# Batched 64x64 matmul: the second half of the transposes moved ahead of the multiplication, and a cast moved from VectorE to GpSimd

## The chip, the cores and the metric

The kernel runs on one core of one Trainium2 chip. The metric is the device time of that core in microseconds (us). All timed runs used below are marked fast, which keeps them apart from runs in a slower state, unless said otherwise. The profile's span is 1.8 to 1.9 us shorter than the device time of the same run.

## The reference

```python
a, b: 1024 x 64 x 64, float32
return np.matmul(a, b).astype(np.float32)
```

That is 16.8 MB for each of a, b and the output: 50.3 MB to be moved for a small amount of arithmetic.

## The kernel before

The batch is cut into 16 b tiles (t, 64 matrices each) and 8 a tiles (s, 128 matrices each). For each tile, a is turned to bf16, transposed on TensorE, spread into a block-diagonal operand on VectorE, and multiplied with b, which is cast to bf16. ScalarE and VectorE copy the results out of PSUM (the memory that TensorE writes to), and GpSimd issues the stores.

Three DMA queues matter. GpSimd's queue (queue 0 of the profile) carries three quarters of each a tile, cast to bf16 by the transfer itself, and all stores. SyncE's queue (queue 1, "SP") carries the fourth quarter in fp32 and the even b tiles, ScalarE's queue (queue 10, "ACT") the odd b tiles.

```python
    def load_a(s):
        a_sb = a_pool.tile([128, 3, 16, 64], bf16, name="a_sb")
        for h in range(3):
            nc.gpsimd.dma_start(out=a_sb[:, h, :, :]..., in_=a_v[s, h])     # casts on the way
        a_raw = a_pool.tile([128, 16, 64], fp32, name="a_raw")
        nc.sync.dma_start(out=a_raw[:]..., in_=a_v[s, 3])
    def load_b(t):                                  # 512-byte pieces in HBM
        queue = nc.scalar if t % 2 else nc.sync
        queue.dma_start(out=b_sb[:], in_=b_v[t])
    def regroup(s):
        # ... (the first a tile is handled apart)
            nc.vector.tensor_copy(a_bf[:, :, 0:3, :], cast_sb[:]...)
            nc.vector.tensor_copy(a_bf[:, :, 3, :], raw[:])
    # ... transpose, spread, cast, multiply, store
    # before the loop: load_first_a(), load_b(0..3), load_a(1), load_a(2)
        for t in range(n_t):
            s, half = t // 2, t % 2
            # ... spread(t + 1), cast(t + 1), load_b(t + 4), load_a(s + 4)
            multiply(t)
            if t == 0:
                regroup(1)
                load_a(A_AHEAD)          # tile 3
                load_a(A_AHEAD + 1)      # tile 4
                transpose(1, 0)
            elif t == 1:
                regroup(2)
            elif half == 0 and s + 2 < n_s:
                regroup(s + 2)
            if half == 0 and s + 1 < n_s:
                transpose(s + 1, 1)
            if half == 1 and s + 2 < n_s:
                transpose(s + 2, 0)
            if t >= HOLD - 1:
                store(t - HOLD + 1)
```

The order is written by hand, and each engine takes its instructions in that order.

Of the kernel before, what the change touches and what calls it, by code (L numbers as in the profile page):

```python
# [13 lines left out]
def kernel(  # L14
# [14 lines left out]
    nc = tc.nc  # L29
# [4 lines left out]
    n_t, n_s = B // 64, B // 128  # L34
# [29 lines left out]
# [4 lines that stand above are left out]
            nc.gpsimd.dma_start(  # L68
                out=a_sb[:, h, :, :].rearrange("p v k -> p (v k)"), in_=a_v[s, h]
            )  # L70
        a_raw = a_pool.tile([128, 16, 64], fp32, name="a_raw")
        nc.sync.dma_start(out=a_raw[:].rearrange("p v k -> p (v k)"), in_=a_v[s, 3])  # L72
        a_tiles[s] = a_sb, a_raw

    def load_first_a():

        raw = [
            o_pool.tile([128, 8, 2, 2, 64], fp32, name="o_sb")[:].rearrange(
                "p gh j wl n -> p (gh j wl n)"
            )  # L80
            for _ in range(2)
        ]
        parts = [raw[h % 2][:, 1024 * (h // 2) : 1024 * (h // 2) + 1024] for h in range(4)]
        for h in range(4):
            (nc.scalar if h % 2 else nc.sync).dma_start(out=parts[h], in_=a_v[0, h])  # L85
        a_tiles[0] = parts

    def load_b(t):
        b_sb = b_pool.tile([128, 16, 128], fp32, name="b_sb")
        queue = nc.scalar if t % 2 else nc.sync  # L90
        queue.dma_start(out=b_sb[:], in_=b_v[t])  # L91
        b_tiles[t] = b_sb

    def regroup(s):
        a_sb = a_tiles.pop(s)
        a_bf = work.tile([128, 16, 4, 64], bf16, name="a_bf")
        if s == 0:
            for h in range(4):
                copy = nc.scalar.copy if h % 2 else nc.vector.tensor_copy
                copy(a_bf[:, :, h, :], a_sb[h].rearrange("p (v k) -> p v k", v=16))  # L100
        else:
            cast_sb, raw = a_sb
            nc.vector.tensor_copy(  # L103
                a_bf[:, :, 0:3, :], cast_sb[:].rearrange("p h v k -> p v h k")
            )
            nc.vector.tensor_copy(a_bf[:, :, 3, :], raw[:])  # L106
        abf_tiles[s] = a_bf
        at_tiles[s] = work.tile([128, 2, 32, 2, 4, 4], fp32, name="at_sb")

    def transpose(s, j):  # L110
        a_cols = abf_tiles[s][:].rearrange("p v h k -> p v (h k)").bitcast(fp32)
        for wl in range(2):
            at_ps = t_psum.tile([128, 4, 128], fp32, name="at_ps")
            for vo in range(4):
                nc.tensor.transpose(  # L115
                    at_ps[:, vo, :], a_cols[:, 4 * vo + 2 * j + wl, :], identity[:]
                )
            nc.scalar.copy(  # L118
                at_tiles[s][:, j, :, wl, :, :],
                at_ps[:].rearrange("p vo (g mp) -> p g mp vo", mp=4),  # L120
            )

    def spread(t):
        half = slice(16 * (t % 2), 16 * (t % 2) + 16)
        bd = bd_tiles[t % N_BD]
        for h in range(4):
            rows = slice(32 * h, 32 * h + 32)
            nc.vector.tensor_copy(  # L128
                bd[rows, :, :, :, h, :].rearrange("p j g wl mo -> p j (g wl) mo"),
                at_tiles[t // 2][rows, :, half, :, :, :].rearrange(  # L130
                    "p j g wl mp vo -> p j (g wl) (mp vo)"
                ),
            )

    def cast(t):
        b_bf = work.tile([128, 16, 128], bf16, name="b_bf")
        b_sb = b_tiles.pop(t)
        if t < n_t - 1:
            (nc.vector.tensor_copy if t else nc.scalar.copy)(b_bf[:], b_sb[:])  # L139
        else:  # L140
            for gq in range(4):
                rows = slice(4 * gq, 4 * gq + 4)
                if gq % 2:
                    nc.vector.tensor_copy(b_bf[:, rows, :], b_sb[:, rows, :])
                else:
                    nc.scalar.copy(b_bf[:, rows, :], b_sb[:, rows, :])  # L146
        bbf_tiles[t] = b_bf
# [5 lines left out]
    def multiply(t):  # L153
        at_bd = bd_tiles[t % N_BD][:].rearrange("p j g wl h mo -> p j g (wl h mo)")
        at_bd = at_bd.bitcast(bf16).rearrange("p j g (c u) -> p j g c u", u=2)
        b_bf = bbf_tiles.pop(t)
        last = t == n_t - 1
        o_sb = o_pool.tile([128, 8, 2, 2, 64], fp32, name="o_sb")

        def put(lo, n):  # L160
            nc.gpsimd.dma_start(  # L161
                out=o_v[t, :, lo : lo + n, :],
                in_=o_sb[:, lo : lo + n].rearrange("p gh j wl n -> p (gh j wl n)"),
            )

        def evacuate(o_ps, gh, n, copies):

            for par in range(2):
                for wl in range(2):
                    src = o_ps[64 * wl : 64 * wl + 64, :, par, :, :]  # L170
                    dst = o_sb[64 * par : 64 * par + 64, gh : gh + n, :, wl, :]
                    copies[2 * par + wl](dst, src)  # L172

        for half in range(2):
            if not last:
                o_ps = o_psum.tile([128, 4, 2, 2, 64], fp32, name="o_ps")
            for g8 in range(8):
                if last and g8 % 4 == 0:
                    o_ps = t_psum.tile([128, 2, 2, 2, 64], fp32, name="at_ps")
                g = 8 * half + g8  # L180
                gl = (g8 % 4 if last else g8) // 2
                for j in range(2):
                    for u in range(2):
                        nc.tensor.matmul(  # L184
                            o_ps[:, gl, g % 2, j, :],
                            at_bd[:, j, g, :, u],
                            b_bf[:, g, 64 * u : 64 * u + 64],
                            start=(u == 0),
                            stop=(u == 1),
                        )  # L190
                if last and g8 % 4 == 3:
                    copy = nc.scalar.copy if g8 == 3 else nc.vector.tensor_copy
                    evacuate(o_ps, g // 4 * 2, 2, [copy] * 4)
            if not last:
                copies = [nc.scalar.copy] * 4
                if half and t % 2:
                    copies[2:] = [nc.vector.tensor_copy] * 2
                evacuate(o_ps, 4 * half, 4, copies)
        if last:
            held[t] = [lambda q=q: put(2 * q, 2) for q in range(4)]  # L200
        else:
            whole = t < n_t - 2
            held[t] = [lambda q=q: put(q, 8 if whole else 4) for q in ([0] if whole else [0, 4])]

    with tc.manual_schedule():
        load_first_a()

        nc.vector.memset(warm[:, 0:1], 0.0)
        nc.scalar.copy(warm[:, 1:2], warm[:, 0:1])  # L209
        load_b(0)  # L210
        load_b(1)
        nc.vector.memset(bd_tiles[0][:], 0.0)  # L212
        make_identity(nc, identity)
        nc.gpsimd.memset(bd_tiles[1][:, 0], 0.0)
        load_a(1)
        load_b(2)
        nc.gpsimd.memset(bd_tiles[1][:, 1], 0.0)  # L217
        load_a(2)
        regroup(0)
        transpose(0, 0)  # L220
        transpose(0, 1)
        load_b(3)
        spread(0)
        cast(0)
        for t in range(n_t):
            s, half = t // 2, t % 2
            if t + 1 < n_t:
                spread(t + 1)
                cast(t + 1)
            if t + B_AHEAD < n_t:  # L230
                load_b(t + B_AHEAD)
            if half == 0 and 0 < s < n_s - 1 - A_AHEAD:
                load_a(s + 1 + A_AHEAD)
            multiply(t)
            if t == 0:
                regroup(1)
                load_a(A_AHEAD)
                load_a(A_AHEAD + 1)
                transpose(1, 0)
            elif t == 1:  # L240
                regroup(2)
            elif half == 0 and s + 2 < n_s:
                regroup(s + 2)
            if half == 0 and s + 1 < n_s:
                transpose(s + 1, 1)
            if half == 1 and s + 2 < n_s:
                transpose(s + 2, 0)
            if t >= HOLD - 1:
                store(t - HOLD + 1)
        for t in range(n_t - HOLD + 1, n_t):  # L250
            store(t)
# [30 lines left out]
```

## Time and profile before

| | before |
|---|---|
| device time, median | 135.62 us |
| span of the profiled run | 133.8 us |
| busy: TensorE, VectorE, ScalarE, GpSimd | 49, 70, 66, 28% of the span |
| bytes in and out | 33.55 + 16.78 MB, 376 GB/s over the span |

The lines of the page that show the bound stand in the prediction. Two more views matter for what happened; I should have weighed them before I predicted. The first is GpSimd's timeline up to 26 us, its DMA issues alone: start, length, engine, line, operation, tiles, count, and in brackets the idle time before it.

```profile
3.00 1.78 POOL L68 DMA_DIRECT2D a_sb<-in_a_dram  x3
...
6.50 2.94 POOL L68 DMA_DIRECT2D a_sb<-in_a_dram  x5
11.65 0.54 POOL L68 DMA_DIRECT2D a_sb<-in_a_dram  x1 [2.21 <-DMA a_sb<-in_a_dram]
23.88 1.61 POOL L68 DMA_DIRECT2D a_sb<-in_a_dram  x3 [11.70 <-DVE a_bf L103]
```

The loads of tile 2, and right behind them those of tile 3 (the last two of the five and the one at 11.65), are issued by 12.2 us, far ahead of their use. And the very first load, issued at 3.00 us on an empty queue 0, has its first packet at 7.11 us by the packets' records, 4.1 us later; the prediction takes no account of that. The second is the table of stretches (its columns head the one in the prediction; the last two are the busy share of the DMA engines and the GB/s that the profile counts).

```profile
5.00:7.00 2.00, 0.00 (x0) 0.00 (x0) 1.82 (x2) 0.23 (x1) 2.00 (x2) 1.00 1.02 416
25.00:28.00 3.00, 3.00 (x27) 2.99 (x25) 0.00 (x0) 2.93 (x6) 0.49 (x1) 1.00 1.07 306
```

From 5 to 7 us queue 0 has not begun, and the two other queues move rows of 4 KB at 416 GB/s. From 25 to 28 us all three queues work; 306 is counted, with the casting loads at their 2 bytes written. By the packets' records, with 4 bytes read, it is 401.

### The profile page before, as it was taken

To read this page: it belongs to the slowest core of one execution; us is meant where nothing else is said; L and a number is where in the kernel's file an instruction comes from. 1 tells how busy PE (TensorE), PEld (TensorE's weight loads), DVE (VectorE), ACT (ScalarE), POOL (GpSimd) and SP (SyncE) were. 2 spreads that over 40 slices of the span, in tenths; PEclk is the share of its full clock that TensorE was granted. 3 is DMA by queue.
4 is the path that set the end of the run, shared out by engine and by line. 5 is a ranking of instruction groups with operands and counts; after the bars stand their busy time and mean duration, and the time that the engine had idled before them with its cause. 6 is when DMAs were issued, how large, how long until landed. Compare 5 with 4: busy or idle time off the path is not lost.

```text
span 133.8 us, 2832 instructions
## 1 busy us (share of the span) xinstructions
PE 65.8 (49%) x1152; PEld 61.6 (46%) x1152; DVE 93.9 (70%) x120; ACT 87.7 (66%) x161; POOL 37.4 (28%) x49
## 2 busy tenths in 40 slices
PE   0005505990078524976398276839535860974000
PEld 0005305990078513966396266738525750963000
DVE  5920299208997039998998999999889949979000
ACT  3134504999137994399779979967994999498000
POOL 8981000420082150307023021404200430426400
PEclk9999999999558965589658977977997798555555
DMA  3999999999999999999999999999999999999991
GB/s 75 359 335 312 305 315 312 306 304 305 306 307 384 365 310 310 393 391 396 317 306 355 403 388 371 318 301 374 393 390 391 393 396 404 404 387 356 337 334 51
DMA packets 17485, 45.01 MB, mean 336 GB/s; under 512 B 1088, under 2 KB 1088, under 8 KB 17472
## 3 DMA queue, kind: packets, MB, share of 16 engines
q0 software_dynamic: 7440, 22.28, 54.8%
q1 hardware_dynamic: 5520, 13.11, 27.0%
q10 hardware_dynamic: 4512, 9.44, 18.6%
q8 instruction: 9, 0.15, 0.4%
q14 instruction: 4, 0.03, 0.1%
HBM read 33.55 MB, written 16.78 MB: 376 GB/s over the span
## 4 chain that ended last, share of the span: by engine, by line
DMA 35%; SPq 27%; ACT 10%; issue 8%; DVE 7%; POOL 3%; PE 3%; POOLq 1%; ACTq 1%; DVEq 0%
SPq L72 23%; DMA a_raw<-in_a_dram 18%; DMA b_sb<-in_b_dram 17%; ACT o_sb L172 8%; DVE at_bd L128 4%; SPq L91 3%; POOL out_dram L161 3%; DVE b_bf L139 3%; PE o_ps L184 3%; ACT at_sb L118 2%; SPq L85 1%; ACT b_bf L146 1%; POOLq L277 1%; ACTq L91 1%; POOLq L161 0%
## 5 line engine op out<-in xcount | busy, mean ns | idle before, releaser
L172 ACT COPY o_sb<-o_ps 64x512 f32<-64x512 f32 x106 | 61.6, 581 | 15.6 <-PE o_ps L184 14.4
L184 PEld LDWEIGHTS <-at_bd 128*128 128x128 bf16 x1024 | 42.8, 114 | 38.0 <-DVE b_bf L139 27.3
L184 PE MATMUL o_ps<-b_bf,at_bd 128*128 128x64 bf16 x960 | 41.2, 214 | 33.3 <-DVE b_bf L139 24.5
L128 DVE COPY at_bd<-at_sb 32x1024 f32<-32x1024 f32 x64 | 45.7, 714 | 16.8 <-ACT at_sb L118 15.1
L161 POOL DMA_DIRECT2D out_dram<-o_sb x20 | 20.3, 1018 | 62.0 <-ACT o_sb L172 24.8
L115 PE MATMUL at_ps<-identity,a_bf 128*128 128x128 f32 x128 | 23.2, 346 | 21.9 <-ACT a_bf L100 11.5
L115 PEld LDWEIGHTS at_ps<-identity,a_bf 128*128 128x128 f32 x128 | 19.7, 184 | 22.1 <-issue 19.3
L118 ACT COPY at_sb<-at_ps 128x512 f32<-128x512 f32 x32 | 17.5, 590 | 8.2 <-PE at_ps L115 7.9
L68 POOL DMA_DIRECT2D a_sb<-in_a_dram x21 | 13.0, 634 | 25.2 <-DVE a_bf L103 19.4
L139 DVE CAST b_bf<-b_sb 128x2048 bf16<-128x2048 f32 x14 | 17.9, 1277 | 1.1 <-DMA b_sb<-in_b_dram 0.7
L172 DVE COPY o_sb<-o_ps 64x512 f32<-64x512 f32 x14 | 9.7, 690 | 0.3
L106 DVE CAST a_bf<-a_raw 128x1024 bf16<-128x1024 f32 x7 | 4.8, 687 | 6.3 <-DMA a_raw<-in_a_dram 6.3
L103 DVE COPY a_bf<-a_sb 128x3072 bf16<-128x3072 bf16 x7 | 6.7, 952 | 0.0
L100 ACT CAST a_bf<-o_sb 128x1024 bf16<-128x1024 f32 x2 | 2.1, 1044 | 5.5 <-DMA o_sb<-in_a_dram 5.5
L139 ACT CAST b_bf<-b_sb 128x2048 bf16<-128x2048 f32 x1 | 1.9, 1898 | 4.0 <-DMA b_sb<-in_b_dram 4.0
L100 DVE CAST a_bf<-o_sb 128x1024 bf16<-128x1024 f32 x2 | 2.5, 1249 | 2.6 <-DMA o_sb<-in_a_dram 2.6
L172 DVE COPY o_sb<-at_ps 64x256 f32<-64x256 f32 x8 | 3.4, 422 | 1.0 <-PE at_ps L184 0.9
L184 PE MATMUL at_ps<-b_bf,at_bd 128*128 128x64 bf16 x64 | 3.6, 242 | 1.0 <-DVE at_bd L128 1.0
L212 DVE MEMSET at_bd<- 128x4096 f32 x1 | 3.5, 3472 | 0.8 <-issue 0.8
L172 ACT COPY o_sb<-at_ps 64x256 f32<-64x256 f32 x8 | 2.9, 367 | 0.1
L209 ACT ACT_TABLE_LOAD x1 | 1.3, 1283 | 2.3 <-issue 2.3
L217 POOL MEMSET at_bd<- 128x2048 f32 x1 | 1.8, 1849 | 0.0
(12 smaller groups left out, 5.6 us busy)
## 6 DMA issues: line engine op xcount, KB each, us to landing
out_dram<-o_sb POOLq DMA_DIRECT2D x14, 1024.0 KB, 22.9
a_sb<-in_a_dram POOLq DMA_DIRECT2D x21, 256.0 KB, 17.8
a_raw<-in_a_dram SPq DMA_DIRECT2D x7, 512.0 KB, 24.1
o_sb<-in_a_dram ACTq DMA_DIRECT2D x2, 512.0 KB, 7.4
o_sb<-in_a_dram SPq DMA_DIRECT2D x2, 512.0 KB, 6.3
out_dram<-o_sb POOLq DMA_DIRECT2D x2, 512.0 KB, 9.4
out_dram<-o_sb POOLq DMA_DIRECT2D x4, 256.0 KB, 8.1
b_sb<-in_b_dram SPq DMA_DIRECT2D x8, 0.5 KB, 22.0
```

The lines of the kernel that those rows point to most:

```text
L68: nc.gpsimd.dma_start(out=a_sb[:, h, :, :].rearrange("p v k -> p (v k)"), in_=a_v[s, h])
L72: nc.sync.dma_start(out=a_raw[:].rearrange("p v k -> p (v k)"), in_=a_v[s, 3])
L91: queue.dma_start(out=b_sb[:], in_=b_v[t])
L103: nc.vector.tensor_copy(a_bf[:, :, 0:3, :], cast_sb[:].rearrange("p h v k -> p v h k"))
L106: nc.vector.tensor_copy(a_bf[:, :, 3, :], raw[:])
L115: nc.tensor.transpose(at_ps[:, vo, :], a_cols[:, 4 * vo + 2 * j + wl, :], identity[:])
L118: nc.scalar.copy(at_tiles[s][:, j, :, wl, :, :], at_ps[:].rearrange("p vo (g mp) -> p g mp vo", mp=4),)
L128: nc.vector.tensor_copy(bd[rows, :, :, :, h, :].rearrange("p j g wl mo -> p j (g wl) mo"), at_tiles[t // 2][rows, :, half, :, :, :].rearrange(
L139: (nc.vector.tensor_copy if t else nc.scalar.copy)(b_bf[:], b_sb[:])
L161: nc.gpsimd.dma_start(out=o_v[t, :, lo : lo + n, :], in_=o_sb[:, lo : lo + n].rearrange("p gh j wl n -> p (gh j wl n)"),)
L172: copies[2 * par + wl](dst, src)
L184: nc.tensor.matmul(o_ps[:, gl, g % 2, j, :], at_bd[:, j, g, :, u], b_bf[:, g, 64 * u : 64 * u + 64], start=(u == 0), stop=(u == 1),)
```

## The change

It takes the casts of the fp32 quarter off VectorE, which is over 90% busy in the middle, and brings both halves of a tile's transposes together, ahead of the even tile's multiplication, so that the block-diagonal copies wait less for them.

```diff
-            nc.vector.tensor_copy(a_bf[:, :, 3, :], raw[:])
+            nc.gpsimd.tensor_copy(a_bf[:, :, 3, :], raw[:])
 ...
+            if half == 0 and 0 < s < n_s - 1:
+                transpose(s + 1, 1)
             multiply(t)
             if t == 0:
                 regroup(1)
                 load_a(A_AHEAD)
                 load_a(A_AHEAD + 1)
                 transpose(1, 0)
+                transpose(1, 1)
 ...
-            if half == 0 and s + 1 < n_s:
-                transpose(s + 1, 1)
```

## The prediction

> **What bounds the kernel now.** I read the page's slices first, to see which resource is full from end to end, then the DMA queues, then the stretches, then the chain and the waits, to see whether any engine's idle time reaches that resource.
>
> ```profile
> DVE  5920299208997039998998999999889949979000
> PEclk9999999999558965589658977977997798555555
> DMA  3999999999999999999999999999999999999991
> GB/s 75 359 335 312 305 315 312 306 304 305 306 307 384 365 310 310 393 391 396 317 306 355 403 388 371 318 301 374 393 390 391 393 396 404 404 387 356 337 334 51
> ...
> q0 software_dynamic: 7440, 22.28, 54.8%
> q1 hardware_dynamic: 5520, 13.11, 27.0%
> q10 hardware_dynamic: 4512, 9.44, 18.6%
> ...
> HBM read 33.55 MB, written 16.78 MB: 376 GB/s over the span
> ## 4 chain that ended last, share of the span: by engine, by line
> DMA 35%; SPq 27%; ACT 10%; issue 8%; DVE 7%; POOL 3%; PE 3%; POOLq 1%; ACTq 1%; DVEq 0%
> ```
>
> The DMA row is what matters: the sixteen DMA engines are over 90% busy in 38 of the 40 slices, all but the first and the last; no compute engine comes near that. The three queues' packet times add to 54.8 + 27.0 + 18.6 = 100.4% of the engines' span. The GB/s row looks uneven, 305 in the first third and 395 later, but that is a matter of counting: queue 0 carries the three quarters of a that are cast on the way, and the profile counts their 2 bytes written, not the 4 read. Loads and stores together are 33.55 + 16.78 = 50.33 MB, the page counts 45.01, and the difference, 5.3 MB, is about the 21 casting loads at 256 KB each. Where queue 0 casts, and each queue gives its share, 305 counted is some 370 to 400 moved. So the byte rate is nearly level.
>
> ```profile
> core 0: us, PE busy (x) PEld busy (x) DVE busy (x) ACT busy (x) POOL busy (x), PEclk, DMA share, GB/s
> ...
> 50.00:65.00 15.00, 9.46 (x152) 8.59 (x150) 13.97 (x19) 10.83 (x21) 3.69 (x4) 0.73 1.05 367
> 65.00:80.00 15.00, 10.48 (x194) 9.72 (x195) 14.16 (x19) 12.26 (x23) 2.86 (x4) 0.73 1.05 356
> ...
> 110.00:120.00 10.00, 5.34 (x97) 5.18 (x98) 8.97 (x12) 7.96 (x15) 2.59 (x3) 0.62 1.03 400
> 120.00:130.00 10.00, 1.85 (x35) 1.69 (x32) 3.38 (x8) 3.31 (x9) 3.60 (x5) 0.50 1.00 345
> ```
>
> This is the table of stretches. VectorE is 93% busy between 50 and 80 us, so one could take it for the bound; but the DMA share is 1.0 or above (packets overlap a little) in every stretch. In the last one the compute engines do next to nothing, and the DMA engines are still full, with stores alone, at 345 GB/s. The timeline of GpSimd has its last store issued at about 124.4 us, 9 us before the end: at some 340 GB/s, and with about 2 us of landing, that is a backlog of some 2.3 MB which was already waiting when the compute ended. A compute that ended some us earlier or later would leave the same bytes to be moved.
>
> **What the Trainium skill says.** (1) "DMA: Bandwidth & Descriptors", section "Queues, rings and completion order": each DMA engine takes its queues in turn, a packet at a time. The trace agrees in its sums: a late or empty queue hands its turns to the others, and the DMA row never drops. (2) The same page, section "Bandwidth", gives about 358 GB/s as one core's HBM share and 435 as the ceiling of the fabric. The trace has 376 over the span and 390 to 404 in mixed slices, so it is above the first and 7% below the second: little is left to be had. (3) "GPSIMD Engine Reference", section "Engine selection": a one-input elementwise operation runs roughly at line rate on GpSimd. The trace has no such copy on GpSimd; its memset of 2048 fp32 took 1.85 us, 0.9 ns an element. (4) "SBUF — State Buffer", section "SBUF: two separate sides": a VectorE instruction in a two-port mode and a GpSimd instruction exclude each other for their whole length. The block-diagonal copies (1024 elements in about 0.69 us) and the casts of b (2048 in 1.23 us) differ by 0.53 ns an element, which I take for that mode; whether they hold GpSimd up no run shows yet.
>
> **The change, part by part.**
>
> ```profile
> L128 DVE COPY at_bd<-at_sb 32x1024 f32<-32x1024 f32 x64 | 45.7, 714 | 16.8 <-ACT at_sb L118 15.1
> L161 POOL DMA_DIRECT2D out_dram<-o_sb x20 | 20.3, 1018 | 62.0 <-ACT o_sb L172 24.8
> ...
> L106 DVE CAST a_bf<-a_raw 128x1024 bf16<-128x1024 f32 x7 | 4.8, 687 | 6.3 <-DMA a_raw<-in_a_dram 6.3
> ```
>
> Each row: busy us and mean ns, then the idle time before and what ended most of it.
>
> *The cast moves.* VectorE loses 7 casts x 0.687 = 4.8 us and a wait of 6.3 us (one: from 42.7 to 48.95 us it stands before the cast of the third a tile, whose load is late). GpSimd gains 7 casts. By the memset, 1024 elements are 0.9 us, with fixed cost 1.1, and up to 2.2 if VectorE's copies hold the port: 8 to 15 us, against 37.4 of 133.8 us busy. By throughput that is free. GpSimd's queue, however, is in order, and the waits come along: the cast of tile 1 now stands ahead of the three casting loads of tile 3 (issued from about 9 us before), and cannot run before its load lands; VectorE ran it at 23.5. So those loads issue at about 25 to 27 us. Queue 0 has the six loads of tiles 1 and 2 before them, 3.1 MB read; at half of 400 GB/s from about 9 us on that lasts until some 25 us. A gap of 0 to 3 us in queue 0 is the result, and the two other queues have work to fill it. The next cast waits for a load used at 36.9 before, so the first store slips from 28.7 to about 38 us; it was queued behind casting loads anyway. The third waits until about 49 us, so the store issued at 39.7 slips to about 50, behind a store and 1.5 MB of loads that keep queue 0 busy past it.
>
> *The transposes move.* Nothing is added: 128 transposes and 32 copies out of PSUM stay. Those of the second half now stand ahead of the multiplication of the even tile, so VectorE's copies, which waited 15.1 us in 6 waits for them, wait less: I take 8 to 10 us off, since the first waits are for loads. In return, each even multiplication stands behind 8 transposes (8 x 0.13 to 0.24 us, 1 to 2 us) and its evacuation behind two more copies of 0.59 us: six times some 2 to 3 us later on TensorE and ScalarE. These cost nothing where the loads decide.
>
> *Sum.* On VectorE, 4.8 + 6.3 + 8 to 10 = about 20 us of work and waits go, of 134. If compute set the end I would have to take off perhaps 10 us. But the sum for the end is the DMA one: about 2.6 us until data flows, 50.33 MB at 376 to 400 GB/s = 126 to 134 us, a last landing of about 2. The change moves no byte, changes no descriptor and no queue. What it can alter is the mix: while stores run beside loads the rate is about 393, stores alone go at 345 at the end. If the loads end 2 us earlier because the compute frees b's buffers earlier, some 0.4 to 0.7 MB more of stores goes at the slow rate: 0.7 / 0.345 - 0.7 / 0.393 = 0.2 us more. If stores come earlier and mix, it is 0.2 us less. Net: 0 to within 0.5 us. I put 135.6 us.
>
> **The rivals.** *(A) VectorE is the true pace, and the kernel gets faster.* For it: 93% busy in the middle, and the chain of waits goes through VectorE, PE and ScalarE from 49 to 65 and from 100 to 113 us. Against it: at that time the DMA row is full, and the chain is mostly DMA and its queue (35 + 27%). It would give 130 to 133 us, no less, since 50.33 MB at 400 GB/s and 4.6 us of ends are 130.4. *(B) GpSimd's casts hold up loads and stores, and the DMA engines run dry.* For it: the order above, and GpSimd's loads and stores wait for earlier transfers too. Against it: transfers take 18 to 24 us from issue to landing, so each queue holds as much in hand, and one queue's gap is another's turn. Should it dry up once at 25 to 30 us and once at 45 to 50, that is 2 to 5 us: 138 to 141. *(C) The lock between GpSimd and VectorE* slows both by up to 7 x 1.5 = 10 us: off the bound too, so under 0.5 us at the end.
>
> **Range and chances.** The before runs lie within 0.05 us, so the spread is that of my argument: 0.5 us for the mix, one small gap of about 1 us upward, one better mix of about 1 us downward. That is 134.5 to 136.9 us. Two per cent are 2.7 us: faster needs rival A nearly to its limit, 0.03; slower needs B, 0.05; within 2%, 0.92.
>
> **What would show it.** Right: the DMA row still 9 from the second slice to the last but one; VectorE's busy time near 89 us, its wait for ScalarE's transposes under 7 us, the 6.3 us wait for the fp32 quarter gone from VectorE and found on GpSimd; GpSimd's cast at 0.9 to 2.2 us; the stretch from 120 to 130 us at 335 to 360 GB/s. Wrong: a DMA slice under 9 between 20 and 60 us (B), or a last store issued after 128 us with the DMA row falling before it. Bytes over span gives the mean rate, 376 GB/s now: over 384 in the changed kernel would say that the mix of loads and stores matters more than I think, and is where I would have been wrong upward.

## The result

| | before | changed |
|---|---|---|
| device time, median | 135.62 us | 137.44 us |
| all runs | 135.51 to 135.66 | 136.81, 137.43, 137.44, 137.44 |
| span of the profiled run | 133.8 us | 134.9 us |

The ratio is 1.0123, with a 95% interval of 1.0095 to 1.0152. Ratios in this document are the mean time of one kernel's fast runs over that of the other's of the same rounds, so they are not quite the ratio of the medians. The change made the kernel 1.2% slower: within 2%, but clear of noise, and outside my range of 134.5 to 136.9. The profiled run of the changed kernel is the quickest of its four.

The same lines of the page as in the prediction, for the changed kernel:

```profile
DVE  5930597019997819998999999797299998963000
DMA  3999999999999999999999999999999999999991
GB/s 80 369 328 310 306 316 312 316 288 305 307 304 306 403 351 308 314 404 395 382 324 311 338 396 400 381 304 307 379 387 392 399 404 399 387 358 340 341 334 57
...
HBM read 33.55 MB, written 16.78 MB: 373 GB/s over the span
...
DMA 49%; SPq 17%; issue 12%; DVE 6%; POOL 4%; PE 2%; ACT 1%; POOLq 1%; DVEq 0%
```

The DMA row is the same as before, 9 in every slice but the first and the last, and yet the mean rate fell from 376 to 373 GB/s. The only mark in the first third is 288 in the ninth slice (27.0 to 30.4 us), which looks harmless beside 305. Then the two groups that the change touches (busy us, mean ns of one, idle before and what ended it):

```profile
L128 DVE COPY at_bd<-at_sb 32x1024 f32<-32x1024 f32 x64 | 50.5, 789 | 14.9 <-ACT at_sb L118 12.4
...
L106 POOL CAST a_bf<-a_raw 128x1024 bf16<-128x1024 f32 x7 | 7.4, 1056 | 33.6 <-DMA a_raw<-in_a_dram 33.6
```

The cast is on GpSimd, 1.06 us each, and GpSimd now stands 33.6 us before it, waiting for the fp32 quarter. VectorE's copies became longer, 789 ns for 714. GpSimd's timeline shows where the longest of those waits is:

```profile
6.48 1.86 POOL L68 DMA_DIRECT2D a_sb<-in_a_dram  x3
22.50 1.12 POOL L106 CAST a_bf<-a_raw 128x1024 bf16<-128x1024 f32 x1 [14.16 <-DMA a_raw<-in_a_dram]
23.56 3.23 POOL L68 DMA_DIRECT2D a_sb<-in_a_dram  x6
```

For 14.16 us GpSimd waits for the first fp32 quarter, and the loads of tile 3 stand behind it: their issue moved from about 8.3 to 23.56 us. And the stretches:

```profile
25.00:28.00 3.00, 2.31 (x49) 2.21 (x48) 0.00 (x0) 2.92 (x7) 1.79 (x4) 1.00 1.05 298
110.00:118.00 8.00, 4.12 (x82) 3.83 (x83) 7.16 (x10) 7.79 (x15) 2.73 (x3) 0.67 1.02 396
120.00:130.00 10.00, 0.69 (x13) 0.53 (x10) 2.42 (x6) 1.33 (x4) 2.85 (x4) 0.50 1.01 344
```

298 against 306 between 25 and 28 us looks like 3%. It is 25%. In the kernel before, half of the traffic in this stretch is casting loads that are counted at half of their size; in the changed kernel there are none, so all is counted. I worked the bytes out from the packets' records, queue by queue, with the casting loads at their size in HBM, the chip's main memory:

```
GB/s moved, in us from the span's start
             24   25   26   27   28   29      queue 0's last packet of tile 2, first of tile 3
before      402  401  402  401  400  390      24.7   24.5
changed     402  317  290  290  346  396      24.8   28.2
```

(Each column is one us.) For 3.4 us queue 0 has nothing to move. SP and ACT have work, their packets follow each other without a pause, and the DMA engines are counted as 1.05 busy; but they move only 290 GB/s. Summed over the columns the changed kernel is 355 KB short of the kernel before, which at 401 GB/s is 0.9 us, of a difference of 1.2 us between the two profiled spans (134.94 and 133.78).

The second, smaller item is at the end. While queue 0 is empty, the loads of the other queues run ahead (0.91 MB of them from 24 to 27 us, before 0.64), so the last load lands sooner (109.1 us, before 110.5), and more stores are left to run alone: 8.34 MB against 7.48. Stores alone begin at some 400 GB/s and fall to 345 (the stretches of 110 to 118 and 120 to 130 us). 0.86 MB at 344 in place of 400 GB/s is 0.35 us. The two estimates add to 1.25 us, against 1.16 measured.

A running total of the same records says where the loss arises. Against the kernel before, the changed kernel is 27 KB ahead at 24 us and 329 KB behind at 30; at 40, 50 and so on to 100 us it is 263 to 342 KB behind, at 110 us 272, and at 125 us 434. So nothing between 30 and 110 us adds to it.

### The profile page after: what moved, and what is told of

It reads as the page before. It is cut to its first block, busy times and chain, and to the rows that moved or that the text cites. A ratio compares the mean times of both kernels' runs of the same rounds, so it can differ in the third digit from the quotient of the medians.

```text
span 134.9 us, 2848 instructions
## 1 busy us (share of the span) xinstructions
PE 63.8 (47%) x1152; PEld 60.6 (45%) x1152; DVE 93.9 (70%) x113; ACT 87.6 (65%) x161; POOL 44.3 (33%) x56
## 4 chain that ended last, share of the span: by engine, by line
DMA 49%; SPq 17%; issue 12%; DVE 6%; POOL 4%; PE 2%; ACT 1%; POOLq 1%; DVEq 0%
DMA a_sb<-in_a_dram 20%; DMA a_raw<-in_a_dram 17%; SPq L72 14%; DMA out_dram<-o_sb 12%; POOL out_dram L161 4%; DVE at_bd L128 3%; SPq L91 2%; DVE b_bf L139 2%; PE o_ps L184 2%; DVE o_sb L172 1%; SPq L85 1%; ACT o_sb L172 1%; POOLq L278 1%; POOL a_sb L68 0%; POOLq L161 0%
## 5 line engine op out<-in xcount | busy, mean ns | idle before, releaser
L128 DVE COPY at_bd<-at_sb 32x1024 f32<-32x1024 f32 x64 | 50.5, 789 | 14.9 <-ACT at_sb L118 12.4
L184 PEld LDWEIGHTS <-at_bd 128*128 128x128 bf16 x1024 | 42.0, 112 | 39.2 <-DVE b_bf L139 23.5
L115 PE MATMUL at_ps<-identity,a_bf 128*128 128x128 f32 x128 | 21.0, 334 | 20.4 <-ACT a_bf L100 10.9
L115 PEld LDWEIGHTS at_ps<-identity,a_bf 128*128 128x128 f32 x128 | 19.0, 178 | 20.7 <-issue 11.9
L106 POOL CAST a_bf<-a_raw 128x1024 bf16<-128x1024 f32 x7 | 7.4, 1056 | 33.6 <-DMA a_raw<-in_a_dram 33.6
L139 DVE CAST b_bf<-b_sb 128x2048 bf16<-128x2048 f32 x14 | 17.2, 1227 | 1.0 <-DMA b_sb<-in_b_dram 0.6
L103 DVE COPY a_bf<-a_sb 128x3072 bf16<-128x3072 bf16 x7 | 7.2, 1023 | 3.5 <-DMA a_sb<-in_a_dram 3.4
```

Source lines behind the costliest of these rows:

```text
L103: nc.vector.tensor_copy(a_bf[:, :, 0:3, :], cast_sb[:].rearrange("p h v k -> p v h k"))
L106: nc.gpsimd.tensor_copy(a_bf[:, :, 3, :], raw[:])
L115: nc.tensor.transpose(at_ps[:, vo, :], a_cols[:, 4 * vo + 2 * j + wl, :], identity[:])
L128: nc.vector.tensor_copy(bd[rows, :, :, :, h, :].rearrange("p j g wl mo -> p j (g wl) mo"), at_tiles[t // 2][rows, :, half, :, :, :].rearrange(
L139: (nc.vector.tensor_copy if t else nc.scalar.copy)(b_bf[:], b_sb[:])
L184: nc.tensor.matmul(o_ps[:, gl, g % 2, j, :], at_bd[:, j, g, :, u], b_bf[:, g, 64 * u : 64 * u + 64], start=(u == 0), stop=(u == 1),)
```

## The experiments

The theory that I took into the experiments (G): the loss comes from the gap in queue 0, which GpSimd's first cast causes by standing before the loads of tile 3; the transposes, and the six later casts, cost nothing. The rivals: the loss comes from the transposes, by way of the stores at the end (T), or from the exclusion between GpSimd's and VectorE's instructions (L).

A correction ahead: in the first two sets of expectations I gave the packets' times 1.8 us too late, because I had not lined them up with the page's clock. Where they say that the gap begins at 26.5 us and that a packet comes 6.3 us after its issue, the right readings are 24.8 us and 4.7 us. Nothing in the verdicts hangs on it, as both ends moved together.

### 1. The transposes alone

```diff
 # changed kernel
-            nc.gpsimd.tensor_copy(a_bf[:, :, 3, :], raw[:])
+            nc.vector.tensor_copy(a_bf[:, :, 3, :], raw[:])
```

> Only the transposes move; the cast of the fp32 quarter stays on VectorE. Theory G (gap): the loss comes from GpSimd's first cast, which stands before the three casting loads of the third a tile and leaves queue 0 empty from about 26.5 to 30 us; without that cast no slice between 20 and 35 us shows a fall, and the time is 135.3 to 136.0 us. Rival T (tail): the loads end earlier because the transposes come earlier, so more stores run alone at some 340 GB/s at the end; then 136.5 to 137.4 us. Rival L (lock, VectorE slowed by GpSimd's casts): 135.3 to 136.0, and the block-diagonal copies are back at about 714 ns.

Measured: 135.47 us against 135.58 for the kernel before on the same chip; ratio 0.9989 (0.9975 to 1.0002). The rate at 25 to 28 us is 402 GB/s by the packets' records. The moved transposes do no harm, and no good that can be told from noise: T falls.

### 2. The casts alone

```diff
 # kernel before
-            nc.vector.tensor_copy(a_bf[:, :, 3, :], raw[:])
+            nc.gpsimd.tensor_copy(a_bf[:, :, 3, :], raw[:])
```

> Only the cast moves to GpSimd; the transposes stay where they were before. G: the whole loss, 136.7 to 137.5 us, and the gap at 26 to 30 us. T: the loads end as before, 135.4 to 136.0 us. L: 136.7 to 137.5 with the copies at about 790 ns, but no fall in the DMA rate at 26 to 30 us.

Measured: 137.31 us, ratio 1.0126 (1.0111 to 1.0141): the whole loss. Queue 0 is empty from 24.9 to 29.2 us, and the records give 315, 290, 290 and 291 GB/s from 25 to 29 us. The two groups:

```profile
L128 DVE COPY at_bd<-at_sb 32x1024 f32<-32x1024 f32 x64 | 49.6, 776 | 22.5 <-ACT at_sb L118 20.7
...
L106 POOL CAST a_bf<-a_raw 128x1024 bf16<-128x1024 f32 x7 | 8.4, 1207 | 31.7 <-DMA a_raw<-in_a_dram 31.7
```

VectorE's copies are slower here as well (776 ns), so this run alone leaves both G and L.

### 3. The changed kernel with the loads of tile 3 first

```diff
 # changed kernel
             if t == 0:
+                load_a(A_AHEAD)
                 regroup(1)
-                load_a(A_AHEAD)
                 load_a(A_AHEAD + 1)
```

> The changed kernel with one line moved: the third a tile's loads are issued ahead of the first tile's cast, so GpSimd still does all seven casts. G: the gap at 26 to 30 us is gone, and with it about 1 us: 135.6 to 136.5 us. T or L: nothing gained, 136.8 to 137.5 us.

Measured: 135.8 us, ratio 1.0006 (0.999 to 1.0021): the loss is gone, but for 0.2% at most. GpSimd still does all seven casts, VectorE's copies still take 778 ns, and GpSimd still waits, now 36.5 us, for the fp32 quarters. But the loads of tile 3 are now ahead of the first of these waits, as its timeline shows:

```profile
6.50 2.93 POOL L68 DMA_DIRECT2D a_sb<-in_a_dram  x5
11.57 0.54 POOL L68 DMA_DIRECT2D a_sb<-in_a_dram  x1 [2.14 <-DMA a_sb<-in_a_dram]
22.62 1.45 POOL L106 CAST a_bf<-a_raw 128x1024 bf16<-128x1024 f32 x1 [10.51 <-DMA a_raw<-in_a_dram]
```

Queue 0 does not run dry, and the records give 402, 402 and 400 GB/s from 25 to 28 us. So L falls, and so does any cost of GpSimd's waits as such.

### 4. The first cast alone

```diff
 # kernel before
-            nc.vector.tensor_copy(a_bf[:, :, 3, :], raw[:])
+            (nc.gpsimd if s == 1 else nc.vector).tensor_copy(a_bf[:, :, 3, :], raw[:])
```

> The kernel before with the first of the seven casts alone on GpSimd. G: this one cast stands before the loads, so nearly the whole loss: 136.3 to 137.4 us with the gap at 26 to 30 us. T: 135.4 to 135.9 us. L: a seventh of the loss, 135.6 to 135.9 us.

Measured: 137.5 us, ratio 1.0138 (1.0122 to 1.0155). One cast of the seven brings the whole loss. From GpSimd's timeline:

```profile
22.84 1.58 POOL L106 CAST a_bf<-a_raw 128x1024 bf16<-128x1024 f32 x1 [14.49 <-DMA a_raw<-in_a_dram]
24.37 3.23 POOL L68 DMA_DIRECT2D a_sb<-in_a_dram  x6
```

The loads of tile 3 issue at 24.37 us, and their first packet moves at 29.3. VectorE's copies are at 713 ns as before, so there is a full loss without their slowing. The two estimates for this run: 427 KB fewer in the gap (1.06 us at 401 GB/s) and 8.88 MB of stores alone, 1.4 MB more than before (0.6 us at some 340 in place of 400 GB/s), together about 1.7 of the 1.8 us between the spans (135.6 and 133.8).

### 5. and 6. No cast at all, but GpSimd kept busy

These hold the loads of tile 3 back by idle work, five or eight memsets, in the kernel before.

```diff
 # kernel before; idle is a scratch tile of 128 x 2048 fp32
                 regroup(1)
+                for _ in range(5):          # or 8
+                    nc.gpsimd.memset(idle[:], 0.0)
                 load_a(A_AHEAD)
```

> The kernel before, with no cast moved, but GpSimd filled with five idle memsets of about 1.85 us ahead of the third a tile's loads, which so issue at about 17.6 us instead of 8.3. In the runs so far the first packet of these loads came about 6.3 us after their issue when queue 0 had run empty, so here it would come at about 24, before queue 0 runs dry at 26.5. Theory G (only an empty queue 0 costs): no gap, 135.3 to 136.0 us. Rival (any delay of GpSimd's loads, or GpSimd's work itself, costs): 136.2 to 137 us.

> The same with eight idle memsets: issue at about 23.2 us, as behind the cast in the changed kernel, first packet at about 29.5. G: the gap from 26.5 to 29.5 us and the whole loss without any cast on GpSimd, 136.7 to 137.6 us. Rival (the cast itself, by its port or its waits): 135.3 to 136.0 us.

Measured: with five, 135.57 us, ratio 1.0 (0.9984 to 1.0017); with eight, 136.97 us, ratio 1.0103 (1.0078 to 1.0128). The timelines of GpSimd, first with five, then with eight:

```profile
8.22 10.15 POOL L239 MEMSET idle<- 128x2048 f32 x5
18.32 2.15 POOL L69 DMA_DIRECT2D a_sb<-in_a_dram  x3
```

```profile
8.21 17.03 POOL L239 MEMSET idle<- 128x2048 f32 x8
25.19 2.15 POOL L69 DMA_DIRECT2D a_sb<-in_a_dram  x3
```

Issued 10 us late, at 18.32, the loads still come in time for queue 0, and nothing is lost. Issued at 25.19, their first packet moves at 29.9 us, the records show 316, 290, 290 and 290 GB/s from 25 to 29 us, and most of the loss is there without any cast on GpSimd. (VectorE's copies are slowed by the memsets, to 817 ns on average, but experiment 4 has the full loss with copies of 713 ns.) What counts is when the loads are issued against the moment at which queue 0 runs dry, not what GpSimd does meanwhile.

In these runs, and in the ones before, an issue on an empty queue 0 is followed by its first packet after 4.7 to 5 us (changed 23.56 and 28.23, casts alone 24.20 and 29.15, first cast 24.37 and 29.26, eight memsets 25.19 and 29.94). The first load of the kernel before took 4.1 us (3.00 and 7.11). In the changed kernel the loads were issued 1.3 us before queue 0 ran dry, and 1.3 us is less than 4.7: the gap of 3.4 us is the difference.

### 7. and 8. b in long pieces

To see why SP and ACT alone move only 290 GB/s, I gave b the same bytes in 8 KB pieces in the kernel before and in the changed one. Their outputs are wrong, which doesn't matter for the times.

```diff
-    b_v = b.rearrange("(t g h) (kp u) n -> t (h kp) g (u n)", h=4, g=16, u=2)
+    b_v = b.rearrange("(t q) (r k) n -> t (q r) (k n)", q=64, r=2)
 ...
-        queue.dma_start(out=b_sb[:], in_=b_v[t])
+        queue.dma_start(out=b_sb[:].rearrange("p g n -> p (g n)"), in_=b_v[t])
```

> The kernel before with b read in 8 KB contiguous pieces per partition instead of 512 B ones; the same bytes into the same tile, so a wrong result on purpose. Reference for the next run: 134.5 to 136 us.

> The changed kernel with b read in 8 KB pieces, wrong result on purpose. If the gap costs because the b loads, left alone with 512 B pieces, move only 290 GB/s instead of 402 (theory P, pieces), then here the rate from 27 to 30 us stays at 380 or above although queue 0 is empty, and the time is within 0.5 us of the run before it. Rival Q (two queues alone cannot fill the engines, whatever the pieces): the rate falls to about 290 to 320 here too, and the time is 1.2 to 2 us above the run before it.

Measured: 134.07 and 134.59 us; ratios to the kernel before 0.9888 (0.9855 to 0.9922) and 0.9923 (0.9899 to 0.9947). This pair did not decide the question. With longer packets the two other queues take a greater share, queue 0 has work of tile 2 until 33 us in place of 25, the first fp32 quarter lands at about 18 (the cast of the changed kernel starts at 18.21), and so there is no gap at all: the rate at 25 to 28 us is 409 to 418 GB/s in both. It shows only that without the gap the changed kernel is some 0.5 us from the other, with intervals that overlap, and that long pieces are worth about 1% here.

### 9. and 10. Queue 0 kept empty at the start

Here the two other queues are alone for longer, by idle work ahead of the first loads of GpSimd, with b in 512 B and in 8 KB pieces. The times are not compared.

```diff
 # kernel before; the second run has the diff of 7 and 8 as well
+        for _ in range(5):
+            nc.gpsimd.memset(idle[:], 0.0)
         load_a(1)
```

> The kernel before with five idle memsets on GpSimd ahead of its very first loads, so that queue 0 is empty until about 17 us and the SP and ACT queues work alone: first on rows of 4 KB (the first a tile), then on b in 512 B pieces. Both theories expect some 415 GB/s while the 4 KB rows go, as in the kernel before at 5 to 7 us. Theory P (the pieces of b are what is slow): about 290 GB/s from 9 us until queue 0 starts. Rival Q (two queues without queue 0 are slow in any case): no step down at the change from a to b. (Times of the packets in my earlier expectations were read 1.8 us late.)

> The same with b read in 8 KB pieces, wrong result on purpose. P: 400 GB/s or more from 9 us until queue 0 starts. Q: about 290 to 320, as in the run with 512 B pieces.

The stretches, first with 512 B pieces, then with 8 KB pieces (nothing casts in them, so the GB/s are true):

```profile
5.00:7.00 2.00, 0.00 (x0) 0.00 (x0) 1.96 (x2) 0.44 (x1) 1.94 (x2) 1.00 1.02 418
9.00:11.00 2.00, 0.31 (x2) 0.34 (x3) 0.49 (x1) 1.04 (x1) 2.00 (x1) 1.00 1.07 296
11.00:13.00 2.00, 2.00 (x11) 2.00 (x10) 0.00 (x0) 0.92 (x2) 1.94 (x2) 1.00 1.04 286
```

```profile
5.00:7.00 2.00, 0.00 (x0) 0.00 (x0) 2.00 (x2) 0.72 (x1) 1.94 (x2) 1.00 1.03 424
9.00:11.00 2.00, 0.00 (x0) 0.00 (x0) 0.48 (x1) 0.92 (x1) 2.00 (x1) 1.00 1.00 424
11.00:13.00 2.00, 1.78 (x9) 1.81 (x10) 0.00 (x0) 0.71 (x2) 1.94 (x2) 1.00 0.99 412
```

In the first row of each, SP and ACT move the 4 KB rows of the first a tile at 418 and 424 GB/s. When they come to b, the rate falls to 296 and 286 with 512 B pieces, and stays at 424 and 412 with 8 KB pieces. The DMA share is 0.99 to 1.07 throughout. Two queues can fill the engines (Q falls); it is b's short pieces, with nothing longer between them, that move at 290 GB/s (P). The other layout changes more than the pieces: by the packets' records b moves in packets of 2,048 bytes with the first and of 8,192 with the second, and the order of addresses differs. Which of these counts, the runs do not separate; "short pieces" stands for all of them here. Why pieces of 512 B are slow alone and do no harm when packets of queue 0 come between them, these runs do not show.

### 11. and 12. Fewer bytes for the last, slow phase

If the second item of the sum is real, a kernel whose stores get more turns earlier should gain. I gave late b tiles to the SP queue, so that ACT's queue is empty for a while and queue 0 is served more often.

```diff
 # changed kernel with the cast on VectorE (experiment 1)
-        queue = nc.scalar if t % 2 else nc.sync
+        queue = nc.scalar if t % 2 and t not in (13,) else nc.sync     # or (9, 13)
```

> The kernel with only the transposes moved, and one late b tile (the fourteenth) loaded on the SP queue in place of the ACT queue, so that ACT's queue is empty for a while, queue 0 gets more turns, and the stores move ahead of the loads. Theory S (the last stores, alone, go at 345 GB/s, so fewer bytes left for that phase cost less time): store bytes after the last load fall from about 7.8 to 7.2 MB, 135.2 us. Without S: no change, 135.5 us, or slower if the later loads hold up the compute.

> The same with two late b tiles (the tenth and the fourteenth) on the SP queue. S: store bytes after the last load about 6.6 MB, 134.9 us. Without S: 135.5 us or slower.

Measured: with one tile moved, 134.89 us against 135.53, ratio 0.996 (0.9945 to 0.9976); with two, 139.7 us, ratio 1.0309 (1.0295 to 1.0323). With one, the last load lands at 114.9 us in place of 109.7, and 5.74 MB of stores are left for the lonely phase in place of 7.78 (I had expected 7.2). The estimate, 2.04 MB at 344 in place of 400 GB/s, is 0.8 us; the two ratios differ by 0.3%, 0.4 us. The direction is as theory S has it, the size half of it. The estimate takes all of these bytes as slow ones, but the rate falls below 400 GB/s only at about 120 us here, 5 us after the last load. The page's DMA row of the run with two tiles moved:

```profile
DMA  3999999999999999999999999999999999924993
```

Here it does show: the last load lands at 119.8 us, the stores in hand are soon done, and the DMA engines idle (2 and 4 in the row) until the last tiles are computed. The backlog of stores at the end hides the compute of the last tiles; it can be made smaller, but not spent. The version with one tile moved is the only one with the right result that beat both kernels: 0.4% under the kernel before. It has the moved transposes, and leaves the cast on VectorE.

## Why the prediction was wrong

*The bound was right.* The DMA engines, not VectorE, set the end. Taking work and waits off VectorE made nothing faster: rival A, whose 130 to 133 us would have been the reward, did not come, neither with the cast nor with the transposes nor with both (experiments 1 to 3). The last store was issued at about 123 us, some 1.6 us earlier than before, and the end came later.

*The order of events on GpSimd was right, and the later slips cost nothing.* The prediction has the first cast ahead of the loads of tile 3, and "A gap of 0 to 3 us in queue 0 is the result". The gap was 3.4 us in the profiled run. The size came out by luck in part: I put the issue at 25 to 27 us, it was 23.56, and I counted no time between issue and first packet, which was 4.7 us. The first two stores slipped much as forecast (28.7 to 36.0 us, where I had 38, and 39.7 to about 48, where I had 50), and the running total of bytes shows no loss there.

*The step that failed is the next clause: "and the two other queues have work to fill it".* The queues did take the turns, but at 290 GB/s and not 402. I took a byte of one queue to be as good as a byte of another. Experiments 9 and 10 show that it is not: b in 512 B pieces with nothing between them is slow. With this, the term that I had at zero in the central figure measures 0.9 us in the profiled run of the changed kernel, and 1.06 to 1.07 us in the runs with the casts alone, the first cast alone and the eight memsets. My range did allow for one small gap of about 1 us, but with 1.3 us above the central figure it had no room for that and the mix in full.

*The term for the mix had the right effect, another cause and about half the size.* I had 0.2 us if loads end earlier, because buffers come free earlier, and 0.4 to 0.7 MB more is stored at the slow rate. The estimate is now 0.86 MB and 0.35 us: more bytes, and 400 GB/s in place of 393 for the stores before the slow phase. The casts alone bring it (8.42 MB), the transposes alone little of it (7.78 against 7.48), so what brought the loads forward was mostly the empty queue.

*Rival B was the right rival with the wrong sign to look for.* I gave 0.05 to a loss of over 2% by it and said that a DMA slice under 9 would show it. No such slice came, because a queue of short pieces keeps the engines counted as busy. The kernel before had the warning in its own profile: the stretch from 5 to 7 us shows two queues at 416 GB/s on 4 KB rows, and no stretch there shows them alone on b; I had no ground for expecting the same rate.

*Of VectorE, most of what I said was off, and it did not matter.* Its busy time stayed at 93.9 us, not 89: 4.8 us of casts left, and its block-diagonal copies grew by 64 x 0.075 = 4.8 us. That the copies grow when GpSimd casts is shown by experiments 1 and 2: 719 ns without its casts, 776 with them. I had expected the exclusion to lengthen GpSimd's casts to 2.2 us; they took 1.06 on average, and VectorE lost instead. The wait for ScalarE's transposes fell from 15.1 to 12.4 us, not to under 7: two waits in the first 30 us, of 5.2 and 7.2 us, make up all of it. In the kernel before the same two were 5.5 and 6.3 us by VectorE's timeline, so only the other four, 3.3 us in all, were within reach of the moved transposes; I had worked from the sum alone. The wait for the fp32 quarter did move from VectorE (6.3 us) to GpSimd, where it is 33.6 us, because GpSimd arrives early.

*What stays open.* The profiled run of the changed kernel took 136.81 us, and its two items explain that. The three others took 137.43 and 137.44, and have no profile. In the runs with 137.3 to 137.5 us of experiments 2 and 4 the first cast took 1.6 us and not 1.12, which put the loads 0.6 to 0.8 us later; that the three runs are of this kind is likely, but not shown. Of the eight memsets' 1.5 us between spans the same two items explain 1.2. Nor do the runs show why lone stores fall from 400 to 345 GB/s some 5 to 8 us after the last load.

## What to carry to other kernels

When an in-order engine also issues transfers, a new instruction on it brings its waits along: look at what stands behind it and issue the loads first (one line moved took the whole loss away). A full DMA row does not say that bytes are moving at full rate: compare bytes, with casting loads at the size that is read, and ask what pieces are left when one queue falls out. Where the end is a backlog of transfers, freeing a compute engine gains nothing, and using the backlog up too far turns the compute of the last tiles into the end.

## What the Trainium skill lacked or had wrong

- "DMA: Bandwidth & Descriptors", section "Specifications", gives 512 B as the least transfer for line rate. Here 512 B pieces with no longer ones between them moved 290 GB/s, the same bytes in 8 KB pieces over 410 (one run each; packets and addresses differ too).
- The same section gives about 1 us to the first byte for transfers issued from GpSimd. Here the first packet came 4.7 to 5 us after the issue on an empty queue, with the two other queues busy, and 4.1 us after it at the start of the kernel before. No page says how early such a load has to be issued to keep a queue from running dry under load.
- "Perfetto Trace Analysis", section "Identifying the Most-Contended Engine", says that occupancy misleads for DMA and to use HBM utilization. The runs agree, and add that a GB/s row that counts what a casting load writes hides the loss as well: 298 against 306 counted was 299 against 401 moved.
- "SBUF — State Buffer", section "SBUF: two separate sides", has the exclusion of VectorE and GpSimd, and gives the shared ports to whichever starts first, while the other waits. The runs agree that they slow each other: VectorE's copies went from 719 to 776 ns. But by the profile's times, which are rough for GpSimd, three copies of the changed kernel that had begun 0.1 to 0.5 us before a cast (at 51.67, 70.54 and 76.38 us) took 1.7 to 2.1 us in place of 0.7, and the casts (at 51.97, 70.63 and 76.90 us) their usual 1.05.
